# Feed-forward down projection: first operands over the gate/up operands that are used up first, and groups of 2, 3, 3, 3 pairs in place of 3, 3, 3, 2

## The chip, the cores and the metric

The kernel runs on one core of a Trainium2 chip. The metric is the device time of one execution in microseconds. Three runs of the kernel before took 2324.43, 2318.01 and 2323.95 us, median 2323.95 us. The core has five engines: TensorE (PE, with its weight loads shown as PEld), VectorE (DVE), ScalarE (ACT), GpSimd (POOL) and SyncE (SP), and 16 DMA engines that serve the queues of SP and POOL. The program holds one list of instructions for each engine, and an instruction can wait for semaphores that other engines or DMAs raise.

## The reference, cut to what matters

One layer of a decoder over 2048 prompt tokens (and 8 single new tokens), model width 1024, feed-forward width 2816. Attention and a gated linear recurrence come first; what is changed lies in the last part:

```
z = rmsnorm(h, ffn_norm_g)
y = h + (silu(z @ w_gate) * (z @ w_up)) @ w_down
```

All in float32. The mids are the product `silu(...) * (...)`, 2048 x 2816.

## The kernel before

The kernel goes through stages one after the other: projections, attention and recurrence, output projection, gate and up ("the way up"), and from about 1861 us of the span on the down projection ("the way down").

Every float32 operand is split into a high and a low part of a narrower kind (`split`, lines 91 to 93: a cast on ACT, line 92, then a subtraction on DVE, line 93), and a product is three matmuls (`mm3`, lines 102 to 106: high by high, high by low, low by high). Matrices are multiplied by Strassen's scheme with seven products, named P1, P6, P2, P7, P5, P4, P3 in the order in which they are computed. The class `Strassen` adds the products up: a product that is finished in PSUM is read by ACT (line 1139, P1) or DVE (line 964) before the bank is used on.

The way up. The operand of each of the seven products on the token side, z0 to z6 (z0 for P1 and so on to z6 for P3; 16512 bytes for each partition), stays in SBUF in the pool `g_zc`, at the right end of the memory, z0 outermost. There are 11 pairs of feature blocks (128 features each), and two halves of tokens. For each pair, seven products for gate and seven for up are computed; in the last pair of the last half the gate products run first and then the up products P1 to P3, so that z0 is read for the last time by the first of the last seven products, and z6 by the very last. The mids, already in the seven sums that the way down needs, are written to DRAM (`md_d`, line 1226) by POOL.

The way down (`group`, from line 1254). The 11 pairs are taken in groups (`GROUPS`, line 38). For a group:
- the rows of `w_down` are loaded (`wrd`, line 1260), and of each pair seven units are made, one for each product (`dhl`, lines 1266 and 1267; sums `tx`, `ty` on DVE, then `split`). A unit takes 4096 bytes of each partition. There are 22 buffers for units, used in turn, so that unit k waits for the last use of unit k - 22.
- for each of eight token tiles (`mi`, two half-tiles of 128 tokens) the mids are loaded by SP (`mr`, line 1300, two buffers of 10752 bytes), split by ACT and DVE into `dm`, and multiplied with the units: 7 products by the group's pairs by 3 matmuls, 63 of them in a group of 3 pairs and 42 in one of 2. In the first tile of each group there are also the few products of the 8 new tokens (`decode`, `ps_ea`, `ps_ec`).
- the four results of a tile are added to `h_d` in DRAM by POOL's accumulating DMA (line 1319), from buffers of which there are two for each result; in the last group they are added on chip to rows of `h_d` loaded again (`hq`, line 1307) and written out (line 1314).

The pools of the way down lie on the memory that `g_zc` has left, so the first write of a tile waits for the last reader of the z operands beneath it. The order of the instructions on each engine comes from a scheduler that simulates the program when it is built; it is fixed at run time. SP's queue holds the loads of the first four blocks of `w_down` rows ahead of the first two loads of mids, and these ahead of the other weight rows.

Of the kernel before, what the change touches and what calls it, by code (L numbers as in the profile page):

```python
# [11 lines left out]
F32R = mybir.dt.float32r  # L12
# [8 lines left out]
P = 128  # L21
# [13 lines left out]
LEVELS = (64, 32, 16, 8, 4, 2, 1)  # L35
NP = NF // 2

GROUPS = ((0, 3), (3, 6), (6, 9), (9, 11))


WIDTHS = (512, 516)
# [10 lines left out]
def hymba_kernel(ctx: ExitStack, tc: tile.TileContext, I, O, X=None, phases=3):  # L52
# [3 lines left out]
    def pool(stack, name, bufs, **kw):  # L56
        return stack.enter_context(tc.tile_pool(name=name, bufs=bufs, reuse_waits="tile", **kw))
# [33 lines left out]
    def split(h, l, src, eng=None):  # L91
        nc.scalar.copy(h, src)  # L92
        (eng or nc.vector).tensor_tensor(l, src, h.bitcast(F32), ALU.subtract)  # L93
# [463 lines left out]
    if phases < 2:  # L557
# [6 lines left out]

    md_d = [[dram.tile([P, 4, 7, p1 - p0, P], F32, name=f"md_d{sb}_{g}") for g, (p0, p1) in enumerate(GROUPS)]
            for sb in range(2)]
# [393 lines left out]
    def sub(out, a, b):  # L960
        nc.vector.tensor_tensor(out, a, b, ALU.subtract)
# [140 lines left out]
    def sums_b(b11, b12, b21, b22):  # L1102

        yield b11
        x, y = (csum.tile([P, 512], F32, tag="s", name=n) for n in ("tx", "ty"))
        sub(x, b22, b12)
        add(y, x, b11)
        yield y
        yield b21
        yield x  # L1110
        sub(x, b12, b11)
        yield x
        sub(y, b21, y)
        yield y
        yield b22
# [40 lines left out]
    with ExitStack() as ph:  # L1156
# [17 lines left out]
        def pair(sb, fp, zc):  # L1174
# [48 lines left out]
            sub(m12, m21, s2)  # L1223
            g = next(g for g, (p0, p1) in enumerate(GROUPS) if p0 <= fp < p1)
            for q, src in enumerate((m11_, s2, m21, s3, s1, m22, m12)):
                nc.gpsimd.dma_start(md_d[sb][g][:, :, q, fp - GROUPS[g][0], :], src.rearrange("p (m t) -> p m t", m=4))  # L1226

# [7 lines left out]


    with ExitStack() as ph:
        wdp = pool(ph, "d_w", 22, side="right")
        mrp = pool(ph, "d_mr", 2, side="right")
        dcp = pool(ph, "d_dec", 1)  # L1240
        pa = pool(ph, "d_ps", 3, space=PSUM)

# [8 lines left out]
        def group(g):  # L1251
            p0, p1 = GROUPS[g]
            npr = p1 - p0
            last = g == len(GROUPS) - 1
            us = []
            for p in range(p0, p1):
                raws = []
                for f in range(2):
                    wr = craw.tile([P, 1024], F32, tag="raw", name="wrd")
                    nc.sync.dma_start(wr, w_d[(2 * p + f) * P:(2 * p + f + 1) * P, :])  # L1260
                    raws.append(wr)
                r0, r1 = raws
                uq = {}
                b = (r0[:, 0:512], r0[:, 512:], r1[:, 0:512], r1[:, 512:])
                for q, src in zip(PRODS, sums_b(*b)):
                    hl = wdp.tile([P, 2, 512], F32R, tag="w", name="dhl")
                    split(hl[:, 0], hl[:, 1], src)
                    uq[q] = hl
                us.append(uq)
# [26 lines left out]
            for mi in range(8):  # L1296
# [25 lines left out]
                for q, name in enumerate(PRODS):  # L1322
                    hl = cu.tile([P, 2, 512], F32R, tag="hl", name="dm")
                    split(hl[:, 0, :npr * P], hl[:, 1, :npr * P], mr[:, q])
                    ps = st.bank(name, 0)
                    for pi in range(npr):
                        cs = slice(pi * P, (pi + 1) * P)
                        w = us[pi][name]
# [5 lines left out]

        for g in range(len(GROUPS)):
            group(g)
# [51 lines left out]
```

## Time and profile before

| | |
|---|---|
| median of 3 runs | 2323.95 us |
| profiled execution | 2326.8 us, its span 2325.0 us |
| mean granted TensorE clock | 0.982 |
| PE busy | 2233.0 us (96%) |
| DVE busy | 1593.4 us (69%) |
| ACT busy | 946.8 us (41%) |
| POOL busy | 637.8 us (27%) |

Times are from the start of the span. A timeline row gives start, length, engine, line, operation, what is written and read, and in brackets how long the engine was idle before it and what ended that. Matmuls overlap in the pipeline: a row of 0.39 us is followed by the next one 0.23 us later. A window row gives the length of the stretch, then busy time and instructions of PE, PEld, DVE, ACT and POOL, the granted clock, the DMA engines' busy share and GB/s.

### The profile page before, as it was taken

Reading aid. Unit: us, or ns where it says so; the run is one execution under the profiler, and the core shown is the slowest. Engines: PE = TensorE matmul, PEld = TensorE weight load, DVE = VectorE, ACT = ScalarE, POOL = GpSimd, SP = SyncE. Lnnn points to the kernel's source line nnn. Section 1 sums busy time; section 2 is a strip of 40 time slices with the busy share of each in tenths; the row PEclk is TensorE's granted clock in tenths of the full one; section 3 lists DMA queues with packets and bytes.
Section 4 is the critical chain, followed back from the end, with each engine's and each line's share of the span. In section 5 each row is a group of like instructions: output and inputs, shape, how many; then the busy total and the mean of one; then the engine's idle time right before and its main releaser. Section 6 shows DMA issues by size and latency. Waiting matters only on the chain.

```text
span 2325.0 us, 34841 instructions
## 1 busy us (share of the span) xinstructions
PE 2233.0 (96%) x12649; PEld 1923.3 (83%) x12649; DVE 1593.4 (69%) x3236; ACT 946.8 (41%) x2120; POOL 637.8 (27%) x807
## 2 busy tenths in 40 slices
PE   8999998899998999799999999999999989999998
PEld 6888886788887877578888889999999958787887
DVE  6787887587866655456666666767676674847477
ACT  5677877343432323223333233333333243534342
POOL 2544544364554133211111110101011122222222
PEclk9999998999998999899999999999999999999999
DMA  7423435255435799882323247323333277878877
GB/s 232 128 91 106 132 107 170 91 182 169 137 108 218 261 330 302 278 275 84 116 87 116 86 147 309 113 88 114 90 101 100 84 218 172 204 167 215 189 192 253
DMA packets 209031, 381.35 MB, mean 164 GB/s; under 512 B 15411, under 2 KB 128332, under 8 KB 202828
## 3 DMA queue, kind: packets, MB, share of 16 engines
q1 hardware_dynamic: 171836, 275.58, 36.2%
q0 software_dynamic: 37024, 103.55, 17.3%
q8 instruction: 100, 1.64, 0.3%
q14 instruction: 71, 0.58, 0.1%
HBM read 219.48 MB, written 160.66 MB: 164 GB/s over the span
## 4 chain that ended last, share of the span: by engine, by line
PE 57%; issue 7%; DMA 7%; DVE 6%; POOL 5%; ACT 1%; SPq 0%; POOLq 0%; ACTq 0%; DVEq 0%
PE ps_b L105 7%; PE ps_b L104 7%; PE ps_b L106 7%; PE ps_c L105 5%; PE ps_c L104 5%; PE ps_c L106 5%; PE ps_a L104 5%; PE ps_a L105 5%; PE ps_a L106 5%; DMA zc_d_P<-zhl 3%; POOL bd L804 2%; DMA z<-zc_d_P 1%; PE ps_v L104 1%; PE ps_v L105 1%; PE ps_v L106 1%
## 5 line engine op out<-in xcount | busy, mean ns | idle before, releaser
L104 PE MATMUL ps_b<-z,whl 128*128 128x258 f32 (+1 forms) x792 | 254.1, 321 | 5.1 <-DMA z<-zc_d_P 5.1
L105 PE MATMUL ps_b<-z,whl 128*128 128x258 f32 (+1 forms) x792 | 254.3, 321 | 0.0
L106 PE MATMUL ps_b<-z,whl 128*128 128x258 f32 (+1 forms) x792 | 253.0, 320 | 0.0
L92 ACT CAST dm<-mr 128x384 fp32r<-128x384 f32 (+1 forms) x224 | 108.0, 488 | 188.7 <-PE ps_b L106 98.1
L104 PE MATMUL ps_a<-z,whl 128*128 128x258 f32 (+1 forms) x528 | 170.6, 323 | 8.6 <-DMA z<-zc_d_P 8.6
L105 PE MATMUL ps_a<-z,whl 128*128 128x258 f32 (+1 forms) x528 | 170.4, 323 | 0.0
L106 PE MATMUL ps_a<-z,whl 128*128 128x258 f32 (+1 forms) x528 | 170.1, 322 | 0.0
L105 PE MATMUL ps_c<-z,whl 128*128 128x258 f32 (+1 forms) x528 | 169.1, 320 | 0.0
L106 PE MATMUL ps_c<-z,whl 128*128 128x258 f32 (+1 forms) x528 | 168.9, 320 | 0.0
L104 PE MATMUL ps_c<-z,whl 128*128 128x258 f32 (+1 forms) x528 | 168.6, 319 | 0.0
L104 PEld LDWEIGHTS ps_b<-z,whl 128*128 128x128 f32 x792 | 149.6, 189 | 17.5 <-DMA z<-zc_d_P 5.6
L106 PEld LDWEIGHTS ps_b<-z,whl 128*128 128x128 f32 x792 | 149.4, 189 | 12.2
L105 PEld LDWEIGHTS ps_b<-z,whl 128*128 128x128 f32 x792 | 149.4, 189 | 12.0
L93 DVE TENSOR_TENSOR dm<-mr,dm 128x384 fp32r<-128x384 f32 (+1 forms) x224 | 115.1, 520 | 60.5 <-ACT dm L92 60.5
L804 POOL TENSOR_TENSOR bd<-E,qTb 64x128 f32<-64x128 f32 x224 | 125.3, 559 | 74.3 <-ACT E L789 59.1
L92 ACT CAST whl<-wrg 128x512 fp32r<-128x512 f32 x132 | 81.6, 619 | 155.9 <-PE ps_b L106 82.9
L93 DVE TENSOR_TENSOR whl<-wrg,whl 128x512 fp32r<-128x512 f32 x132 | 90.9, 689 | 42.4 <-ACT whl L92 42.1
L1226 POOL DMA_DIRECT2D md_d<-m x22 | 15.6, 710 | 378.1 <-DVE m L1189 364.7
L964 DVE TENSOR_TENSOR gu<-ps_c,gu 128x512 f32<-128x512 f32 (+1 forms) x130 | 78.1, 600 | 60.0 <-PE ps_c L106 59.3
L104 PEld LDWEIGHTS ps_a<-z,whl 128*128 128x128 f32 x528 | 100.7, 191 | 17.6 <-issue 4.7
L105 PEld LDWEIGHTS ps_a<-z,whl 128*128 128x128 f32 x528 | 100.3, 190 | 8.1
L106 PEld LDWEIGHTS ps_a<-z,whl 128*128 128x128 f32 x528 | 100.2, 190 | 7.8
(386 smaller groups left out, 6626.3 us busy)
## 6 DMA issues: line engine op xcount, KB each, us to landing
mr<-md_d SPq DMA_DIRECT2D x24, 1344.0 KB, 7.0
zc_d_P<-zhl POOLq DMA_DIRECT2D x49, 512.0 KB, 8.4
wrg<-in_w_gate_dram SPq DMA_DIRECT2D x44, 512.0 KB, 4.0
wrg<-in_w_up_dram SPq DMA_DIRECT2D x44, 512.0 KB, 11.8
nT_d<-nT SPq DMA_DIRECT2D x16, 1024.0 KB, 6.0
zT<-nT_d SPq DMA_DIRECT2D x8, 2048.0 KB
mt<-mix_d SPq DMA_DIRECT2D x16, 1024.0 KB, 8.0
z<-zc_d_P SPq DMA_DIRECT2D x7, 2064.0 KB, 19.8
```

The lines of the kernel that those rows point to most:

```text
L92: nc.scalar.copy(h, src)
L93: (eng or nc.vector).tensor_tensor(l, src, h.bitcast(F32), ALU.subtract)
L104: nc.tensor.matmul(ps, lh, rh, start=start, stop=False, skip_group_check=more)
L105: nc.tensor.matmul(ps, lh, rl, start=False, stop=False, skip_group_check=more)
L106: nc.tensor.matmul(ps, ll, rh, start=False, stop=stop, skip_group_check=more)
L804: nc.gpsimd.tensor_tensor(bv[rows, :, h], eo, qo, ALU.mult)
L964: nc.vector.tensor_tensor(out, a, b, ALU.add)
L1226: nc.gpsimd.dma_start(md_d[sb][g][:, :, q, fp - GROUPS[g][0], :], src.rearrange("p (m t) -> p m t", m=4))
```

## The change

Two things in one. The groups of pairs become 2, 3, 3, 3. And the pools at the right end are opened in another order: the two buffers of mids first, then the 22 buffers for units, now as two pools of 8 and 14 that are still used in turn as one ring.

```diff
-GROUPS = ((0, 3), (3, 6), (6, 9), (9, 11))
+GROUPS = ((0, 2), (2, 5), (5, 8), (8, 11))
...
-        wdp = pool(ph, "d_w", 22, side="right")
         mrp = pool(ph, "d_mr", 2, side="right")
+        wdps = (pool(ph, "d_wa", 8, side="right"), pool(ph, "d_wb", 14, side="right"))
+        made = [0]
...
-                    hl = wdp.tile([P, 2, 512], F32R, tag="w", name="dhl")
+                    hl = wdps[made[0] % 22 >= 8].tile([P, 2, 512], F32R, tag="w", name="dhl")
+                    made[0] += 1
```

By the addresses of the two built programs: before, the two mids buffers lay over z6 and z5, so that the first mids load waited for the last matmul of the way up; the first units lay over z5 and then z0, z1 and so on. After, the mids buffers lie over z0 and z1, whose last readers are the first two of the seven up products (P1 and P6), the first eight units over z1, z2 and z3, the ninth (P6 of the second pair) over z6, and the next ones over z3 and z4. Nothing ahead of the last up products moves. The lines below the change are 2 to 3 higher in number.

The scheduler sets the order anew from there. On ACT, at the end of the way up (`dhl` are units, `dm` the split mids, `mdec` the new tokens' mids), before:

```order
L1217 COPY mdec<-gp_17957 128x4
L92 CAST dhl<-wrd 128x512
L92 CAST dhl<-ty 128x512
L92 CAST dhl<-wrd 128x512
L92 CAST dhl<-tx 128x512
L1217 COPY mdec<-gu_17958 128x4
L92 CAST mhl<-mdec 128x22x8
L92 CAST dm<-mr 128x384 x7
L92 CAST dhl<-tx 128x512
```

and after, at the same place:

```order
L1217 COPY mdec<-gp_17957 128x4
L92 CAST dhl<-wrd 128x512
L92 CAST dhl<-ty 128x512
L92 CAST dhl<-wrd 128x512
L92 CAST dhl<-tx 128x512
L92 CAST dhl<-ty 128x512
L92 CAST dhl<-wrd 128x512
L92 CAST dhl<-tx 128x512
L1217 COPY mdec<-gu_17958 128x4
L92 CAST dm<-mr 128x256 x4
L92 CAST mhl<-mdec 128x22x8
L92 CAST dm<-mr 128x256 x3
```

Three units of the second pair have come ahead of the mids; the first of these three is the one over z6. On DVE, from the first unit's subtraction (right behind the last sum of the way up) to the first of the mids, before (`up`, `uu`, `gu` are the last pair's sums of mids):

```order
L93 TENSOR_TENSOR dhl<-wrd,dhl 128x512
L964 TENSOR_TENSOR up_17960<-gu_17958,gu_17959 128x512
L961 TENSOR_TENSOR uu_17962<-m_17956,gu_17958 128x512
L93 TENSOR_TENSOR dhl<-ty,dhl 128x512
L93 TENSOR_TENSOR dhl<-wrd,dhl 128x512
L961 TENSOR_TENSOR uu_17961<-up_17960,m_17956 128x512
L93 TENSOR_TENSOR dhl<-tx,dhl 128x512
L93 TENSOR_TENSOR mhl<-mdec,mhl 128x22x8
L961 TENSOR_TENSOR ty<-wrd,ty 128x512
L961 TENSOR_TENSOR gu_17958<-gp_17957,uu_17961 128x512
L961 TENSOR_TENSOR tx<-wrd 128x512
L93 TENSOR_TENSOR dm<-mr,dm 128x384 x7
```

and after:

```order
L93 TENSOR_TENSOR dhl<-wrd,dhl 128x512
L964 TENSOR_TENSOR up_17960<-gu_17958,gu_17959 128x512
L961 TENSOR_TENSOR uu_17962<-m_17956,gu_17958 128x512
L93 TENSOR_TENSOR dhl<-ty,dhl 128x512
L93 TENSOR_TENSOR dhl<-wrd,dhl 128x512
L961 TENSOR_TENSOR uu_17961<-up_17960,m_17956 128x512
L93 TENSOR_TENSOR dhl<-tx,dhl 128x512
L93 TENSOR_TENSOR dhl<-ty,dhl 128x512
L93 TENSOR_TENSOR dhl<-wrd,dhl 128x512
L961 TENSOR_TENSOR ty<-wrd,ty 128x512
L93 TENSOR_TENSOR dhl<-tx,dhl 128x512
L93 TENSOR_TENSOR dm<-mr,dm 128x256 x2
```

Eleven rows stand ahead of the mids in both. On DVE the whole of the first tile's preparation is shorter after: in place of 21 units and mids of 384 columns there are 14 units and mids of 256 columns ahead of the second tile's.

## Rows read from the trace of the kernel before

**Rows 1.** Windows: us, busy time (instructions) of each engine, clock, DMA share, GB/s

```profile
1860.00:1870.00 10.00, 3.62 (x14) 2.54 (x13) 9.42 (x19) 5.06 (x13) 3.70 (x5) 0.71 0.89 323
1870.00:1880.00 10.00, 7.26 (x23) 3.79 (x22) 9.32 (x17) 5.43 (x11) 0.00 (x0) 0.84 0.96 377
1880.00:1890.00 10.00, 8.36 (x32) 5.39 (x31) 7.40 (x13) 6.12 (x13) 0.92 (x1) 0.94 0.17 54
...
1995.00:2018.00 23.00, 23.00 (x103) 17.21 (x102) 20.80 (x36) 11.86 (x24) 4.29 (x6) 1.00 0.85 214
```

**Rows 2.** Waits of PE from 1700 us on: total us, times, longest

```profile
PE ps_a L104 <- ACT dm L92: 6.4, 1, 6.4
PE ps_c L104 <- ACT dhl L92: 2.2, 1, 2.2
```

**Rows 3.** Timeline of PE, 1858 to 1900 us: start, length, engine, line, what

```profile
1860.51 0.28 PE L106 MATMUL ps_c<-z,whl 128*128 128x258 f32 x1
1867.18 0.79 PE L104 MATMUL ps_a<-dhl,dm 128*128 128x512 f32 x1 [6.38 <-ACT dm L92]
...
1877.39 0.50 PE L104 MATMUL ps_c<-dhl,dm 128*128 128x512 f32 x1 [2.22 <-ACT dhl L92]
...
1890.07 0.39 PE L104 MATMUL ps_b<-dhl,dm 128*128 128x512 f32 x1
...
1894.38 0.39 PE L106 MATMUL ps_b<-dhl,dm 128*128 128x512 f32 x1
```

**Rows 4.** Timeline of SP's queue, 1840 to 1905 us

```profile
1860.82 0.80 SPq L1300 DMA_DIRECT2D mr<-md_d  x2
```

**Rows 5.** Timeline of ACT, 1840 to 1905 us

```profile
1858.97 0.62 ACT L92 CAST dhl<-wrd 128x512 fp32r<-128x512 f32 x1
1859.49 0.61 ACT L92 CAST dhl<-ty 128x512 fp32r<-128x512 f32 x1
...
1866.61 2.99 ACT L92 CAST dm<-mr 128x384 fp32r<-128x384 f32 x7 [4.24 <-DMA mr<-md_d]
```

**Rows 6.** Timeline of DVE, 1840 to 1905 us

```profile
1846.51 0.43 DVE L964 TENSOR_TENSOR uu<-ps_b,up 128x258 f32<-128x258 f32 x1 [1.02 <-PE ps_b L106]
...
1861.63 0.69 DVE L93 TENSOR_TENSOR dhl<-wrd,dhl 128x512 fp32r<-128x512 f32 x1
1862.23 0.69 DVE L964 TENSOR_TENSOR up<-gu,gu 128x512 f32<-128x512 f32 x1
...
1883.70 0.69 DVE L961 TENSOR_TENSOR tx<-wrd 128x512 f32<-128x512 f32 x1 [2.50 <-DMA wrd<-in_w_down_dram]
...
1889.22 0.69 DVE L964 TENSOR_TENSOR gu<-ps_b,gp 128x512 f32<-128x512 f32 x1
```

**Rows 7.** Timeline of DVE in the last group, of 2 pairs

```profile
2270.19 0.75 DVE L93 TENSOR_TENSOR dm<-mr,dm 128x256 fp32r<-128x256 f32 x2
```

**Rows 8.** Windows with the low clock, columns as in rows 1

```profile
1878.00:1879.00 1.00, 1.00 (x3) 0.69 (x3) 1.00 (x3) 0.90 (x2) 0.00 (x0) 0.50 0.89 283
```

**Rows 9.** DMA from 1920 to 1995 us: queues (packets, MB, share), then issues (KB, landing)

```profile
q0 software_dynamic: 3114, 5.66, 48.9%
q1 hardware_dynamic: 1010, 7.93, 31.6%
...
mr<-md_d SPq DMA_DIRECT2D x5, 1344.0 KB, 8.0
h_d<-gu POOLq DMA_DIRECT2D x11, 256.0 KB, 4.9
wrd<-in_w_down_dram SPq DMA_DIRECT2D x3, 512.0 KB
h_d<-gp POOLq DMA_DIRECT2D x5, 256.0 KB, 7.1
h_d<-c POOLq DMA_DIRECT2D x5, 256.0 KB, 5.4
```

**Rows 10.** All accumulating DMAs into `h_d`: us from issue to landing

```profile
DMA to landing us min/median/max: 2.7/5.6/9.8
```

## The prediction

> **What bounds the kernel now.** I read the page first: PE is busy 96% of the span, so only a place where PE waits or runs slowly can pay. Then the table of windows, for the stretch that the change touches [rows 1]: from 1860 to 1890 us PE is busy for only 3.62 + 7.26 + 8.36 = 19.24 of 30 us, with a granted clock of 0.71, 0.84 and 0.94, while DVE is busy nearly without a break until 1880. At the next change of group PE is busy 23 of 23 us, at full clock [rows 1]. So the loss lies at the start of the way down and hardly anywhere else. The list of PE's waits names two of its parts: 6.4 us for the first mids and 2.2 us for a unit [rows 2].
>
> The timelines show the chain. The last up matmul starts at 1860.51 and the first matmul of the way down at 1867.18, after 6.38 us [rows 3]. SP issues the mids load at 1860.82, right behind that last matmul, since the buffer lies over z6 [rows 4]. ACT sits idle for 4.24 us until it has landed, and splits from 1866.61 [rows 5]. From then on PE is fed in drips, because DVE has 21 units, their sums and the first mids to go through from 1861.63 on; its first read of a finished product in PSUM comes at 1889.22, after a wait of 2.50 us for weight rows at 1883.70 [rows 6].
>
> To have one number for this start, I take the time at which a PE that ran at full pace from its first matmul on would have had to begin. The pace is (1894.38 - 1890.07) / 19 = 0.227 us for each instruction [rows 3], the first and last of 20 such rows. From 1867.18 up to 1890.07, 58 instructions had been started. So the start counts as 1890.07 - 58 x 0.227 = 1876.9. Against the end of the way up (about 1861) some 16 us are lost.
>
> **The change part by part.** The number of matmuls, splits, loads and accumulations is the same; there is again one group of 2 pairs. Nothing is gained by work removed, only by order and waits.
>
> 1. Mids first. Their buffers now lie over z0 and z1, free after the up product P6, whose second piece DVE reads at 1846.51 [rows 6]. SP's queue holds nothing else at that time, so the load goes out at about 1846.5 in place of 1860.82 and, at the 6 us that it took there (1860.82 to 1866.61 [rows 4, 5]), lands near 1852. That wait goes. What is late next is ACT: after its four casts of units, 0.52 us apart from 1858.97 on [rows 5], come three more, the first of which waits for z6, so for the end of the way up (about 1861.1, when ACT gets there anyway). Seven casts end near 1862.7, a small copy and the first cast of mids at about 1863.1. PE starts then, 4.1 us earlier.
>
> 2. DVE's list. This sets the pace, and the early mids do not help it: eleven rows stand ahead of the first mids, each 0.60 us after the one before [rows 6], so 1861.63 + 11 x 0.60 = 1868.2. In the old order too the mids came only after eleven such rows, when they had landed. What gets shorter is the list itself. Up to the first read of a finished product there are now 14 units of the first group and one of the next, 4 sums, 4 rows that end the last pair (23 x 0.60 = 13.8), one short row (0.25) and 8 mids of 256 columns, 0.33 us apart [rows 7] (2.6): 16.7 us, so until 1878.3 in place of 1889.22.
>
> 3. What PE does meanwhile. In its new order 35 instructions stand ahead of the first product that reuses a bank; they are let go one by one by those DVE rows, the last of them at about 1877. Eleven more need nothing new and bring PE to 46 at 1879.6. That counts as a start at 1879.6 - 46 x 0.227 = 1869.2. DVE stays the busier engine for a while: walking both lists on with the same distances, PE waits 0.9 us at its next reuse of a bank near 1884 and 0.8 us near 1893, and the start counts as 1870.9. From there on DVE's load falls, since only 8 units of the next group have a free buffer. Gain so far: 1876.9 - 1870.9 = 6.0 us.
>
> 4. The clock. Before, after the gaps of 6.38 and 2.22 us [rows 3] the granted clock stood at 0.50 [rows 8], the lower of the two levels (1.2 in place of 2.4 GHz), at which the pace is 0.454 in place of 0.227 us. The drips remain, so part of this will stay. While PE waits for DVE it costs nothing. If the low clock lasts from 1875.9, when the instructions come close together, to 1881.2, where it ended before (0.94 of the ten us from 1880 on [rows 1] leave 1.2 us at half the clock), 5.3 us hold 11.7 instructions in place of 23.3, which costs 11.6 x 0.227 = 2.6 us. At best nothing. I take 0.8, nearer to nothing, since PE is busy for more than half of the time from 1871 on.
>
> 5. The first group's tiles. In a group of 3 pairs, a tile has 63 matmuls, 63 x 0.227 = 14.3 us; in the first group now 42, 9.5 us, while the four accumulations into `h_d` stay. From 1920 to 1995 us, 21 accumulations took 48.9% of 75 us, 1.75 us each; on the other queue 5 loads of 1344 KB and 3 of 512 KB took 31.6%, 23.7 us, or 2.87 us for 1000 KB [rows 9]. A tile of 2 pairs needs 4 x 1.75 + 0.896 x 2.87 = 9.6 us of DMA, just what it has. In the old order the 2-pair group was the last, which loads and stores in place of accumulating. Each result has two buffers: between the last matmul of P3 in one tile and P7 two tiles later, which waits until the sum buffer has been written out, stand 48 matmuls, 10.9 us. In them fit DVE's addition (0.69), POOL's issue (0.85), the landing, DVE's next addition (0.69) and about 1 us of hand-overs: 3.2 us beside the landing. With the median landing of 5.6 us [rows 10] that is 8.8, with the longest of 9.8 it is 13.0, so 2.1 us too long; six tiles depend on it: between nothing and 13 us. The landings of one result have a median of 4.9, those of another 7.1 us [rows 9], so I take little more than nothing, 0.2 us for each of six, 1.2 us.
>
> 6. The last group now has 3 pairs. Its loads and stores have more time for each tile. PE waits there hardly at all before, and the last products and stores come in the same way: nothing, 1 us either way.
>
> Sum: 6.0 - 0.8 - 1.2 = 4.0 us. The profiled execution takes 2326.8 us, so 2322.8; it lies 2.85 us above the median of the runs, 2323.95, and from that I forecast 2320.0 us.
>
> **The rivals.**
>
> *The drips keep the clock low.* For it: [rows 8], and that PE still waits for DVE some 15 us long. Against it: from 1880 on the mean was 0.94 [rows 1], though PE still waited here and there. Term 4 at its bound: 6.0 - 2.6 - 1.2 = 2.2 us, 2321.8 us. The Trainium skill, page "TensorE: Matmul & The Clock Gate", section "A second HAM failure mode: psum-queue depth-cycling", says that a PE which idles a little and often between groups of matmuls goes back and forth between the two clocks and loses throughput by it. By that rule this rival would be the likeliest; the trace agrees for the gaps of 2 us and more and shows no case of gaps as small as those that I expect.
>
> *Only DVE's list counts.* The waits after 1879.6 don't come, the clock stays up and the DMAs keep pace: 1876.9 - 1869.2 = 7.7 us, 2316.3 us. For it: from 1890 on PE hardly waits before, with DVE as busy as here. If DVE's list were not binding either, PE would run on from 1863.1: 13.8 us, 2310.2 us. Against that stands the order: 11 rows of 0.60 us come ahead of the first mids.
>
> *Given back at the next group.* The 21 units of the second group must be made while a group of 8 x 9.5 = 76 us runs, not 115 us, and 13 of them have to wait for buffers of the first. Before, DVE was busy 20.80 of 23 us at such a change without a wait of PE [rows 1]; some 4 us more would make it the bound: 2324 us, no change.
>
> *The first group becomes bound by its accumulations* (slower). Term 5 at its bound: each of six tiles loses 2.1 to 2.2 us, 13 us against 5.2: 2332 us. It decides from a landing of 7.7 us on, and landings of `gp` have a median of 7.1 already [rows 9]. Against it: the waiting slows the stream of accumulations down, so that the queue empties.
>
> **How the numbers follow.** Forecast 0.40; low clock 0.15; only DVE's list 0.24; given back 0.13; accumulations 0.08. Faster by over 0.3% (7 us; a measurement of this kernel, whose three runs lie 6 us apart, can tell no less from no change) come out of the third case and a little of the first: 0.26. Slower by as much: the last, 0.08. Within: 0.66. The range from 2312 to 2330 us takes in 12 us of gain, near the bound of 13.8, and most of the loss by accumulations.
>
> **What would show it right or wrong.** In the new profile: the mids load issued near 1846.5; PE's first matmul of the way down near 1863; DVE without a break from 1861.6 to about 1878 and its first read of a product near 1878.5; PE's pace close to full from about 1880. The start, counted as above, lies near 1871. Accumulations in the first group land in 6 to 8 us. I am wrong if PE waits for sums of P6 or P4 tile after tile before 1950, if it waits at the change to the second group, or if the start is done before 1866.

## The result, and the profile after

The changed kernel is slower, not faster: 2328.32 us median of 7 runs (2326.15 to 2334.56), against 2321.47 us for the kernel before (2318.01 to 2324.43, 7 runs). The ratio is 1.0029, 95% interval 1.0016 to 1.0042. Forecast were 2320.0 us, with 2312 to 2330 us as the range.

The profiled execution took 2327.4 us (span 2325.6). Its span hardly differs from before (2325.0), because its way up ended 6 us earlier, at 1854.28 in place of 1860.51 us; that end lies anywhere from 1854 to 1863 us in the profiles below, whatever the way down looks like. So the two must be laid side by side from that end on: from the last up matmul to the last matmul of all it is 457.3 us before and 464.1 us after, 6.8 us more.

Here is the table of windows of the changed kernel (us, then for PE, PEld, DVE, ACT and POOL busy time and instructions, clock, DMA share, GB/s), for comparison with [rows 1]:

```profile
1854.00:1864.00 10.00, 3.53 (x13) 2.28 (x12) 9.41 (x20) 4.95 (x14) 3.32 (x5) 0.72 0.31 105
1864.00:1874.00 10.00, 9.96 (x35) 6.14 (x34) 9.48 (x20) 7.10 (x15) 0.38 (x1) 0.77 0.84 279
1874.00:1884.00 10.00, 10.00 (x45) 7.87 (x44) 9.85 (x19) 5.45 (x12) 2.93 (x4) 1.00 0.56 103
1884.00:1904.00 20.00, 18.68 (x80) 14.48 (x79) 15.79 (x32) 8.22 (x20) 7.21 (x10) 1.00 0.98 243
1904.00:1940.00 36.00, 36.00 (x161) 29.80 (x160) 21.77 (x47) 12.79 (x33) 13.79 (x17) 1.00 0.98 216
1940.00:1980.00 40.00, 34.57 (x144) 24.35 (x143) 30.53 (x54) 19.30 (x39) 8.16 (x10) 1.00 0.77 191
2074.00:2094.00 20.00, 18.26 (x72) 12.60 (x71) 15.42 (x27) 9.19 (x19) 2.55 (x3) 0.91 0.83 226
```

The third ten us are full, where before 8.36 of ten were. But PE now has gaps where it had none: in the first group, at its end (busy for 34.57 of 40 us), and at the second change of group.

To put numbers on this I went through the starts of PE's 1936 matmuls of the way down. Where two follow each other by more than 0.3 us, the distance less the pace of 0.227 us counts as lost. Sums by time since the start of the last up matmul, one profiled execution each:

| kernel | way down, us | 0-30 | 30-60 | 60-130 | 130-180 | 180-260 | later | time against before (95%) |
|---|---|---|---|---|---|---|---|---|
| before | 457.3 | 16.0 | 0 | 0 | 0 | 0 | 1.6 | 1 |
| changed | 464.1 | 10.3 | 2.1 | 7.2 | 0 | 4.1 | 0.4 | 1.0029 (1.0016-1.0042) |
| changed, again (e9) | 463.6 | 10.2 | 3.1 | 6.3 | 0 | 3.8 | 0 | 1.0028 (1.0017-1.0039) |
| new places only (e1) | 459.2 | 13.7 | 0 | 0 | 2.3 | 0 | 3.1 | 1.0009 (0.9997-1.0021) |
| new groups only (e2) | 462.1 | 9.2 | 6.0 | 3.1 | 0 | 2.6 | 1.4 | 1.0018 (1.0006-1.0030) |
| first group not stored (e3) | 452.7 | 10.4 | 0 | 0 | 0 | 2.5 | 0 | 0.9986 (0.9975-0.9997) |
| small group third (e4) | 461.6 | 13.8 | 0 | 0 | 2.3 | 0 | 5.2 | 1.0025 (1.0015-1.0036) |
| four buffers (e5) | 454.8 | 11.8 | 1.2 | 0 | 0 | 0.3 | 1.9 | 0.9981 (0.9970-0.9991) |
| new groups, four buffers (e6) | 459.0 | 9.2 | 4.2 | 0 | 0 | 4.2 | 1.4 | 1.0002 (0.9991-1.0013) |
| plain stores (e7) | 456.2 | 10.3 | 1.4 | 2.0 | 0 | 2.4 | 0.1 | 0.9986 (0.9973-0.9998) |
| two groups not stored (e8) | 450.7 | 10.4 | 0 | 0 | 0 | 0 | 0.5 | 0.9973 (0.9962-0.9985) |
| before, four buffers (e10) | 461.6 | 15.4 | 0 | 0 | 0 | 0 | 6.2 | 1.0004 (0.9992-1.0016) |
| seven splits on POOL (e11) | 460.7 | 14.1 | 1.6 | 0.9 | 0 | 2.4 | 1.7 | 1.0016 (1.0005-1.0027) |
| five splits on POOL (e12) | 462.1 | 14.3 | 2.0 | 1.3 | 0 | 2.5 | 2.1 | 1.0014 (1.0004-1.0024) |

The columns explain the result: the start gains 5.7 us (16.0 to 10.3), and 13.8 us are lost behind it, where before 1.6 were. The edge at 30 us cuts through the start in e2 and e6, where PE waits for DVE's first splits until 32 us and more. Counted up to 37 us, the start loses 16.0 us before, 10.9 in the changed kernel, 13.7 in e1, 12.9 in e2, 12.1 in e5 and 11.3 in e6. One execution and the median of 7 to 12 runs agree within some 2 us, in e10 within 4.

The start first, in the timelines of PE, SP and DVE (start, length, what, and idle time before it with what ended it):

```profile
1854.28 0.28 PE L106 MATMUL ps_c<-z,whl 128*128 128x258 f32 x1
1856.92 0.50 PE L104 MATMUL ps_a<-dhl,dm 128*128 128x512 f32 x1 [2.36 <-ACT dm L92]
...
1862.49 0.80 PE L106 MATMUL ps_a<-dhl,dm 128*128 128x512 f32 x1 [4.05 <-DVE dm L93]
...
1868.71 0.39 PE L105 MATMUL ps_c<-dhl,dm 128*128 128x512 f32 x1
...
1869.86 0.39 PE L105 MATMUL ps_a<-dhl,dm 128*128 128x512 f32 x1
```

```profile
1840.20 0.98 SPq L1303 DMA_DIRECT2D mr<-md_d  x2
```

```profile
1855.40 0.69 DVE L93 TENSOR_TENSOR dhl<-wrd,dhl 128x512 fp32r<-128x512 f32 x1
...
1869.44 0.42 DVE L93 TENSOR_TENSOR dm<-mr,dm 128x256 fp32r<-128x256 f32 x1
...
1872.18 0.68 DVE L964 TENSOR_TENSOR gu<-ps_b,gp 128x512 f32<-128x512 f32 x1
```

The mids' load goes out 14 us before the end of the way up ([rows 4]: 0.3 us after it), and PE's first matmul follows 2.64 us after the last up matmul ([rows 3]: 6.67). Then PE stands for 4.05 us until DVE has split the first mids: the one wait is gone and another has taken most of its place, since DVE comes to the mids only after its unit splits. DVE's first read of a finished product comes 1872.18 - 1855.40 = 16.8 us after it begins its list ([rows 6]: 27.6 us).

Now the first group's end. ACT copies the first product of a tile (`gp`) and must wait for the accumulation of the one two tiles back:

```profile
1921.30 0.59 ACT L1139 COPY gp<-ps_a 128x512 f32<-128x512 f32 x1 [4.98 <-DMA h_d<-gp]
...
1930.39 0.59 ACT L1139 COPY gp<-ps_a 128x512 f32<-128x512 f32 x1 [4.55 <-DMA h_d<-gp]
1930.87 1.77 ACT L92 CAST dm<-mr 128x256 fp32r<-128x256 f32 x5
...
1935.63 0.63 ACT L92 CAST dhl<-ty 128x512 fp32r<-128x512 f32 x1 [0.27 <-PE ps_a L106]
1940.66 0.59 ACT L1139 COPY gp<-ps_a 128x512 f32<-128x512 f32 x1 [4.40 <-DMA h_d<-gp]
1941.14 0.41 ACT L92 CAST dm<-mr 128x256 fp32r<-128x256 f32 x1
1941.45 0.62 ACT L92 CAST dhl<-wrd 128x512 fp32r<-128x512 f32 x1
```

At 1930 the wait costs PE nothing: only a few casts of mids are queued behind it. At 1940 the casts of the second group's units are queued there too, and DVE's rows wait for those. DVE's timeline shows it:

```profile
1941.59 0.43 DVE L93 TENSOR_TENSOR dm<-mr,dm 128x256 fp32r<-128x256 f32 x1 [4.14 <-ACT dm L92]
...
1955.42 0.56 DVE L93 TENSOR_TENSOR dm<-mr,dm 128x384 fp32r<-128x384 f32 x1
1959.43 0.69 DVE L961 TENSOR_TENSOR tx<-wrd 128x512 f32<-128x512 f32 x1 [3.45 <-DMA wrd<-in_w_down_dram]
...
1972.91 0.69 DVE L961 TENSOR_TENSOR tx<-wrd 128x512 f32<-128x512 f32 x1 [4.02 <-DMA wrd<-in_w_down_dram]
```

DVE is idle 4.14 us, then busy 14 us without a break, during which PE waits for it piece by piece (3.4 us). The splits that free the staging buffers of weight rows are late as well, so the next weight loads are issued late (the first 92.8 us after the end of the way up, against 86.3 in e3, where the first group has no accumulations) and DVE waits for them twice; that costs PE another 3.8 us, in two gaps near 1962 and 1976 us.

The wait hands itself on from tile to tile. Between ACT's copy at 1921.30 and the next one at 1930.39 stand DVE's addition of P4 of the tile before and POOL's store of that `gp` (first the last matmul of this P4 on PE):

```profile
1920.02 0.39 PE L106 MATMUL ps_b<-dhl,dm 128*128 128x512 f32 x1
```

```profile
1923.52 0.68 DVE L964 TENSOR_TENSOR gp<-ps_b,gp 128x512 f32<-128x512 f32 x1
```

```profile
1924.50 0.85 POOL L1322 DMA_DIRECT2D h_d<-gp  x1 [4.30 <-DVE gp L964]
```

DVE was idle before that, because its rows wait for casts that stand behind the copy on ACT; P4 itself had been finished since about 1920.4 (1920.02 + 0.39). So a late copy makes the next store late, and that store the next copy: 2.2 us from the copy to DVE's addition, 1.0 to the issue, 5.9 until the buffer is back, 9.1 us in all. The rounds before and after it, from copy to copy, took 9.5 and 10.3 us. A tile of 42 matmuls takes PE 9.5 us, so a delay that has once come in is hardly made up.

At the second change of group DVE waits for weight rows once more, and PE loses 4.1 us behind that wait, 1.6 of them at the low clock (eight matmuls 0.43 us apart; the window above shows a mean of 0.91):

```profile
2076.87 0.69 DVE L961 TENSOR_TENSOR tx<-wrd 128x512 f32<-128x512 f32 x1 [3.66 <-DMA wrd<-in_w_down_dram]
```

### The profile page after: what moved, and what is told of

Read it like the earlier page. It is cut to its first block, busy times and chain, and to the rows that moved or that the text cites. A ratio compares the mean times of both kernels' runs of the same rounds, so it can differ in the third digit from the quotient of the medians.

```text
span 2325.6 us, 34835 instructions
## 1 busy us (share of the span) xinstructions
PE 2232.7 (96%) x12649; PEld 1920.6 (83%) x12649; DVE 1591.6 (68%) x3236; ACT 944.2 (41%) x2120; POOL 639.5 (27%) x807
## 4 chain that ended last, share of the span: by engine, by line
PE 64%; issue 11%; DMA 10%; DVE 8%; POOL 6%; ACT 2%; SPq 0%; POOLq 0%; ACTq 0%; DVEq 0%
PE ps_b L105 6%; PE ps_b L104 6%; PE ps_b L106 6%; PE ps_a L104 4%; PE ps_a L105 4%; PE ps_a L106 4%; PE ps_c L105 4%; PE ps_c L104 4%; PE ps_c L106 4%; DMA zc_d_P<-zhl 3%; PE ps_d L104 3%; PE ps_d L105 3%; PE ps_d L106 3%; POOL bd L804 2%; DMA z<-zc_d_P 1%
## 5 line engine op out<-in xcount | busy, mean ns | idle before, releaser
L106 PEld LDWEIGHTS ps_b<-z,whl 128*128 128x128 f32 x792 | 149.3, 188 | 12.1
L104 PEld LDWEIGHTS ps_a<-z,whl 128*128 128x128 f32 x528 | 100.9, 191 | 19.6 <-issue 6.5
L964 DVE TENSOR_TENSOR gu<-ps_b,gp 128x512 f32<-128x512 f32 (+1 forms) x130 | 77.8, 598 | 46.0 <-PE ps_b L106 40.0
L105 PEld LDWEIGHTS ps_a<-z,whl 128*128 128x128 f32 x528 | 100.3, 190 | 8.1
## 6 DMA issues: line engine op xcount, KB each, us to landing
wrg<-in_w_up_dram SPq DMA_DIRECT2D x44, 512.0 KB, 11.8
```

The source lines that it names most:

```text
L104: nc.tensor.matmul(ps, lh, rh, start=start, stop=False, skip_group_check=more)
L105: nc.tensor.matmul(ps, lh, rl, start=False, stop=False, skip_group_check=more)
L106: nc.tensor.matmul(ps, ll, rh, start=False, stop=stop, skip_group_check=more)
L964: nc.vector.tensor_tensor(out, a, b, ALU.add)
```

## The experiments

Theory A: what costs time is the small first group, through its accumulations. Its rivals: the ring split into two pools (B), the 21 units that must be made in a short time whatever the accumulations do (C), the closeness to the start (D).

**e1, new places, old groups.**

```
-GROUPS = ((0, 2), (2, 5), (5, 8), (8, 11))
+GROUPS = ((0, 3), (3, 6), (6, 9), (9, 11))
```

> The new places of mids and units with the old groups of 3, 3, 3, 2 pairs. Theory A (the loss sits behind the start: the small first group has only 9.5 us for a tile, its accumulations and the next group's units get too little time): nothing is lost later, and the start gains little, since VectorE has 21 units to go through as before; 0 to 3 us faster than the kernel before, TensorE's waits after the first 40 us of the way down at most 2 us in all. Theory B (the split of the ring into two pools makes later units and loads late): about 7 us slower than the kernel before, with waits of 3 us and more at the later changes of group.

Measured: 1.0009 (0.9997 to 1.0021), not told from no change. A's 0 to 3 us of gain didn't come. The start loses 2.3 us less than before, and nothing is lost from 30 to 130 us, as A expected. But 5.4 us are lost later, more than the 2 us that A allowed and less than B wanted: 3.1 of them at the changes of group (the kernel before lost 0.5 there), the rest in the last group, 1.1 of it at its end as in the kernel before.

**e2, new groups, old places** (the kernel before with the new line `GROUPS`).

> The new groups of 2, 3, 3, 3 pairs with the old places of mids and units. Theory A: the 6 us wait for the first mids stays, the later losses of some 12 us come as in the changed kernel; 6 to 12 us slower than the kernel before. Theory B: the later losses don't come; no slower than the kernel before, at best 5 us faster, since VectorE's list at the start is shorter.

Measured: 1.0018 (1.0006 to 1.0030), some 4 us slower; the later losses are there. B falls as the main cause: they come with the groups, not with the places. From 37 to 130 us 5.4 us are lost, against 8.7 in the changed kernel, and ACT waits for accumulations here too. The size is a miss for A (6 to 12). One reason is the start, which is better than that of the kernel before though the mids' wait is there with 5.5 us: up to 37 us it loses 12.9 us, against 16.0 before and 10.9 with both changes.

**e3, first group's accumulations left out** of the changed kernel, 32 of 256 KB each (the number in the expectation is a slip).

```
-                    nc.gpsimd.dma_start(h_d[ti][:, cols], c, accum_op=ALU.add)
+                    if g:
+                        nc.gpsimd.dma_start(h_d[ti][:, cols], c, accum_op=ALU.add)
```

> The changed kernel, with the accumulations of the first group into h_d left out (64 of 64 KB rows of work for the DMA queues less; everything is still computed). Theory A with accumulations as the cause: ScalarE no longer waits for their landing (21 us in the changed kernel), the waits of TensorE up to 1955 us (5.5 us) go and those for late weight rows behind it (3.8 us) shrink; 5 to 9 us faster than the changed kernel. Theory C (the 21 units of the next group in a short time are too much for VectorE and for the weight loads, whatever the accumulations do): within 2 us of the changed kernel, the waits from 1943 to 1977 us stay.

Measured: 0.9986 (0.9975 to 0.9997), some 10 us below the changed kernel, a little more than A's 5 to 9. Both columns from 30 to 130 us go to zero, so C falls: the same 21 units in the same time cost nothing. DMA's part in it, from windows of this kernel:

```profile
1904.00:1940.00 36.00, 36.00 (x160) 29.84 (x159) 23.82 (x49) 14.31 (x34) 0.00 (x0) 1.00 0.39 125
1940.00:1980.00 40.00, 40.00 (x176) 31.00 (x176) 33.74 (x61) 20.85 (x41) 4.18 (x5) 1.00 0.51 162
```

The DMA share is 0.39 where it was 0.98. That alone doesn't tell whether the DMA engines were too full or a single accumulation too slow to come back; e5 does.

**e4, small group third.** `GROUPS = ((0, 3), (3, 6), (6, 8), (8, 11))`, else the changed kernel.

> The new places, with groups of 3, 3, 2, 3 pairs: the small group is the third. Theory A: the start is that of the new places with the old groups; the losses of some 7 us appear in and behind the small group, about 250 to 360 us into the way down; 4 to 8 us slower than the kernel before. Theory D (the losses come because the first group runs into the tail of the start, not because it is small): no waits there, within 2 us of the kernel before.

Measured: 1.0025 (1.0015 to 1.0036), 5.8 us slower: D falls, and the size is in A's range. The place is not: 4.7 us are lost in the first half of the small group, from 260 to 300 us, and hardly anything at its end. ACT waited 18.6 us there for accumulations, as in the small first group. So where such waits turn into a loss depends on what is queued behind them.

**e5, four buffers.** The changed kernel, in which every second tile uses the result tiles of the up product:

```
-                st = Strassen(Pd(), 512, ((0, 512),), "g", done)
+                st = Strassen(Pd(), 512, ((0, 512),), "g" if last or mi % 2 == 0 else "u", done)
```

> The changed kernel, but each of three results (those of the sums p1, u2, u3) has four buffers in place of two in the groups that accumulate: every second tile uses the tiles of the up product, which lie idle there. No DMA is saved. Theory A1 (what costs is the hand-back of the two buffers, that is the latency of an accumulation, 5 to 8 us): the 9 us that TensorE loses between 30 and 130 us after the end of the way up shrink to under 2, as with the accumulations left out; 5 to 9 us faster than the changed kernel, up to 4 faster than before. Theory A2 (what costs is the DMA engines' throughput, their share near 1.0 in the first group): the loss only moves, since the queue gets longer: within 3 us of the changed kernel.

Measured: 0.9981 (0.9970 to 0.9991), 4.4 us faster than before and some 11 faster than the changed kernel, a little more than the 5 to 9 of A1: the version that beats both. From 30 to 130 us 1.2 us are lost in place of 9.3. The windows of this kernel:

```profile
1884.00:1904.00 20.00, 19.44 (x84) 15.42 (x83) 17.49 (x35) 10.29 (x24) 7.68 (x9) 1.00 0.78 195
1904.00:1940.00 36.00, 35.90 (x158) 29.77 (x159) 24.09 (x50) 13.23 (x33) 14.52 (x17) 1.00 1.05 239
1940.00:1980.00 40.00, 40.00 (x177) 31.19 (x176) 33.91 (x61) 21.14 (x42) 11.06 (x13) 1.00 0.86 225
```

The DMA engines are as full as in the changed kernel (1.05 and 0.98) and move more (239 and 216 GB/s), and an accumulation takes no less time to land: the issues from 1890 to 1950 us, changed kernel first, then four buffers (KB each, median us to landing):

```profile
h_d<-gu POOLq DMA_DIRECT2D x13, 256.0 KB, 5.9
h_d<-gp POOLq DMA_DIRECT2D x6, 256.0 KB, 6.0
```

```profile
h_d<-gu POOLq DMA_DIRECT2D x7, 256.0 KB, 7.0
h_d<-gp POOLq DMA_DIRECT2D x4, 256.0 KB, 7.4
```

So it was the hand-back of two buffers (A1), not the throughput (A2). The same copy on ACT now waits for PE alone, 0.87 us:

```profile
1931.62 0.59 ACT L1139 COPY gp<-ps_a 128x512 f32<-128x512 f32 x1 [0.87 <-PE ps_a L106]
```

**e6, new groups, old places, four buffers** (the same line in the kernel of e2).

> The same four buffers, with the new groups but the old places of mids and units. If the new places are worth nothing once the first group has 2 pairs (start 9.3 us lost with the old places, 10.3 with the new ones), this is within 2 us of the changed kernel with four buffers; if they are worth the 6 us of the mids' wait, it is 4 to 6 us slower than that.

Measured: 1.0002, about 4.9 us more than e5. By the letter the new places would be worth that. The table says where: the first 60 us lose 13.4 us here and 13.0 in e5, so next to nothing at the start; 3.9 us lie at the second change of group.

**e7, plain stores in the first group.** The accumulation of `g == 0` becomes `nc.gpsimd.dma_start(h0_d[ti][:, cols], c)`.

> The changed kernel, with plain stores of the first group into a buffer of their own in place of accumulations: the first group's part is left out of the result; buffers, instructions and bytes written stay. If the price is the reading and adding of an accumulation (1.75 us of all DMA engines for each), the loss between 30 and 130 us (9.3 us) falls to under 3 us; if any store of that size through GpSimd's queue is as slow, it stays above 6.

Measured: 0.9986 (0.9973 to 0.9998); 3.4 us are lost from 30 to 130 us, near the lower of the two bounds. ACT still waits for stores (11.0 us from 1870 to 1980), which land in a median of 4.5 (`gu`) to 5.4 us (`gp`), where accumulations took 5.9 and 6.0. So most of the loss hangs on 0.6 to 1.4 us of landing: the buffers come back just too late, not far too late. Of the last two rounds from copy to copy here, one took 8.4 us, less than a tile's 9.5, and one 9.7; ACT's waits shrink from tile to tile (3.80, 2.69 and 2.01 us, where the changed kernel had 4.98, 4.55 and 4.40).

**e8, second group's accumulations left out too** (`if g > 1:`).

> The changed kernel, with the accumulations of the first and the second group left out. It asks for the 2.5 to 4 us that are lost at the second change of group, 200 to 230 us after the end of the way up, with the first group's accumulations or without them. If weight rows land late there because accumulations fill the DMA engines: that loss goes, 2 us faster than with the first group alone left out. If the load is issued late, behind splits that free its buffer: it stays.

Measured: 0.9973 (0.9962 to 0.9985), 3 us below e3; the loss at the second change is gone. DVE waits 0.2 us for the weight rows where in e3 it waits 3.7 (e3 first):

```profile
2073.93 0.69 DVE L961 TENSOR_TENSOR tx<-wrd 128x512 f32<-128x512 f32 x1 [3.70 <-DMA wrd<-in_w_down_dram]
```

```profile
2072.39 0.69 DVE L961 TENSOR_TENSOR tx<-wrd 128x512 f32<-128x512 f32 x1 [0.22 <-DMA wrd<-in_w_down_dram]
```

The load was issued 206.2 us after the end of the way up in both. From there to its landing (KB, us), e3 first:

```profile
wrd<-in_w_down_dram SPq DMA_DIRECT2D x1, 512.0 KB, 6.9
```

```profile
wrd<-in_w_down_dram SPq DMA_DIRECT2D x1, 512.0 KB, 3.4
```

So there it is not the issue but the landing, which is slower beside accumulations. The kernel before has a wait of 2.9 us at its second change too, and PE lost 0.5 us by it. In e5, which loses 0.3 us there, the same load took 5.5 us; in e6, which loses 4.2, it took 8.7, with the same accumulations. Why is not settled; their orders differ a little everywhere.

**e9, the changed kernel again.**

> The changed kernel once more, for a second profile and times on the same chip as the next three. If the losses are a matter of its order and buffers, the same waits come back: start some 10 us, 30 to 130 us some 9 us, second change of group 2.5 to 4 us, and 5 to 9 us slower than the kernel before. If they were an accident of one execution, some of these are absent.

Measured: 1.0028, and the same losses in the same columns. They belong to the program, not to one execution.

**e10, the kernel before with four buffers.**

> The kernel before with four buffers for each of the three results. With 14.3 us for a tile the two buffers came back in time (ScalarE never waits for an accumulation there), so nothing is to be gained: within 2 us of the kernel before. If four buffers are worth something by themselves, it is 3 us faster or more, and the gain of the changed kernel with four buffers does not come from the change.

Measured: 1.0004 (0.9992 to 1.0016): nothing gained where a tile lasts 14.3 us. The expectation overstates one thing: in the kernel before ScalarE waits for an accumulation twice in the whole way down, 2.2 and 2.3 us, without a loss for PE in that stretch. The profile of e10 shows some 6 us lost in the last group, where the kernel before loses 1.1; the runs' times don't show that much, and its cause stays open.

**e11 and e12, splits moved to POOL** in the kernel of e5 (e12 with the condition `and q in ("P2", "P7", "P5", "P4", "P3")` added):

```
-                    split(hl[:, 0], hl[:, 1], src)
+                    split(hl[:, 0], hl[:, 1], src, nc.gpsimd if g == 0 and p == p0 + 1 else None)
```

> The changed kernel with four buffers, and the subtractions of the second pair's seven first units moved from VectorE to GpSimd (1.31 us each there by a like row of the kernel before, 9.2 us in all). If VectorE's list sets the start, as the prediction said, its first read of a finished product comes up to 4 us sooner after the end of the way up (16.8 us in the run with four buffers) and the start loses 2 to 4 us less: 2 to 4 us faster than with four buffers alone. If something else sets it (GpSimd's slower rows, the clock), it is within 1 us or slower.

> As the run with seven, but the first two of the pair stay on VectorE and five go to GpSimd (6.5 us). VectorE's list is shorter by 3 us; if GpSimd's rate limits the run with seven, this one is the faster of the two, else it is 1 us slower.

Measured: 1.0016 and 1.0014, both some 8 us slower than e5; the start loses 14.1 and 14.3 us in place of 11.8. DVE's list got shorter by rows, not by time. DVE, then POOL, in e11:

```profile
1861.34 5.53 DVE L93 TENSOR_TENSOR dhl<-ty,dhl 128x512 fp32r<-128x512 f32 x1
1866.80 0.68 DVE L93 TENSOR_TENSOR dhl<-wrd,dhl 128x512 fp32r<-128x512 f32 x1
```

```profile
1861.77 1.35 POOL L93 TENSOR_TENSOR dhl<-ty,dhl 128x512 fp32r<-128x512 f32 x1
1862.98 0.82 POOL L1226 DMA_DIRECT2D md_d<-uu  x1
1863.67 1.43 POOL L93 TENSOR_TENSOR dhl<-wrd,dhl 128x512 fp32r<-128x512 f32 x1
1864.89 1.43 POOL L93 TENSOR_TENSOR dhl<-tx,dhl 128x512 fp32r<-128x512 f32 x1
```

A split that takes 0.69 us elsewhere took 5.53 us while POOL worked through three of its own, the last of which ended at 1866.3. In e11 DVE's first read of a product came 19.5 us after the begin of its list, not sooner than e5's 16.8 but 2.7 us later, and the start lost 2.3 us more. That fits a list that sets the start, but it is no test of it, since POOL's splits came late as well.

## Why the prediction was wrong, point by point

- **Mids first (step 1): right in its times.** First matmul 2.6 us after the last up matmul, as forecast. That the early mids are worth nothing by themselves, as step 2 said, is not borne out as it stands: e1, with the new places alone, loses 2.3 us less at the start. Beside the new groups they are worth 2.0 us (12.9 in e2, 10.9 in the changed kernel, up to 37 us) or, with four buffers, less than nothing (11.3 in e6, 12.1 in e5).
- **DVE's list (step 2): right.** Forecast 16.7 us to the first read of a product, measured 16.8.
- **What PE does meanwhile, and the clock (steps 3 and 4): right in the sum.** Forecast a gain of 6.0 - 0.8 = 5.2 us at the start, measured 5.7. PE ran at half its pace for a while (0.43 us apart up to 1868.4, [rows 8] before), but at 1869.86, at full pace again, its matmul began as DVE's split of the mids ended (1869.44 + 0.42). So DVE was the one waited for, and the 0.8 us for the clock are not seen.
- **The first group's tiles (step 5): this is the step that failed.** It named the cause, gave it 0 to 13 us and took 1.2; measured are 9.3 (e3: 0, e5: 1.2). It followed one buffer, `gu`, through one pass, from the last matmul of P3 to P7 two tiles later. Its 48 matmuls are those of the changed program's order from the fourth tile on (the code's order would give 60), so the count was not the mistake. The mistake is the term for DVE: the sum lets DVE add as soon as a product is finished and charges 0.69 us. In the trace DVE adds P4 2.8 to 3.5 us after that (before the last three of ACT's waits), because the addition stands behind rows that wait for the copy of P1, and that copy waits for the buffer of `gp`. The prediction's own buffer was nearly as tight: DVE waited for `gu` once, 1.5 us at 1904. So the terms close to a round that comes back in every tile: 9.1 to 10.3 us with landings of 5.8 to 6.9, where a tile has 9.5. In one pass the same landings would hold ACT up for 0.4 to 1.5 us: from the last matmul of P4 to the end of P1 two tiles later stand 20 to 28 matmuls, 28 or 6.4 us for the last three tiles, against 6.8 to 7.9 us for addition, issue and landing. The order on ACT and DVE, from which the round follows, could have been read before the result.
- **Why the late copy cost what it did.** It took no time from PE while little stood behind it on ACT (1904 to 1940 us: 36.00 of 36), 2.1 us in the first tiles, and 7.2 when the next group's units stood behind it. My rival put the loss at 13 us from landings of 7.7 us on and gave it 0.08. Its cause was the right one, and it set in at 6. Its price was not: it charged some 2 us for each of six tiles, and the tiles themselves lost little. That the loss came near its size is in part luck.
- **The next groups.** Step 5 looked at the first group alone, and "given back at the next group" priced DVE's load (4 us) with a chance of 0.13. The load is there, but it costs nothing by itself (e3). The wait at the change to the second group, one of the prediction's signs of being wrong, did come, through the late copy. The 4.1 us at the second change of group are in no step.

Of the 12.2 us lost more behind the start, some 8 are shown to be the buffers' hand-back: from 30 to 130 us the changed kernel loses 9.3, e5 1.2 and e3 nothing, and four buffers alone gain nothing (e10). At the second change of group e8 shows the weight rows' landing beside the second group's accumulations (2.5 us in e3, nothing in e8); why that costs 4.1 us in the changed kernel and 0.3 in e5 stays open.

## What to carry to other kernels

Where a piece of work gets smaller and its results go out by DMA, follow each buffer once round in the planner's order on every engine, not in one pass but from one use to the next: copy, addition, issue, landing, copy again. If the addition stands on its engine behind rows that wait for the last hand-back, the times add up to a round, and the round must be shorter than the piece of work. A wait on a helper engine that costs nothing for many tiles gets its price from what is queued behind it; look at the last tile before a change of phase. More buffers out of tiles that lie idle can be worth more than the change itself: four buffers turned +0.29% into -0.19%.

## What the runs showed of the hardware

- VectorE and GpSimd can keep each other out: one 128x512 subtraction on VectorE took 5.53 us in place of 0.69 while GpSimd ran three of its own of 1.35 to 1.43 us (e11), and it ended 0.55 us after the last of them. The Trainium skill, page "SBUF — State Buffer", section "SBUF: two separate sides", says that the two share a pair of ports as an exclusive lock: the instruction that starts first has it for its whole length, and the other is blocked. The trace agrees that one was blocked while the other worked. It does not bear out which one: VectorE's row began first (1861.34 against 1861.77 us), and it was held over three rows of GpSimd.
- An accumulation of 256 KB through GpSimd's queue landed in a median of 6.0 us (`gp`, first group), a plain store of the same size in 5.4. With four buffers the median was 7.4 us, and more was moved in all (247 in place of 225 GB/s from 1890 to 1950 us).
- The same load of 512 KB landed 6.9 us after its issue beside accumulations (e3) and 3.4 us without them (e8).
